# Weight splits of a float32 decoder trunk: low halves on GpSimd in four pieces, all high halves on ScalarE

## The chip, the cores and the metric

The kernel runs on one core of a Trainium2 chip. The metric is the device time of one execution in microseconds (us); the time given for a kernel is the median of its runs. Engines are named as in the profile: PE is TensorE's matmul and PEld its weight load, DVE is VectorE, ACT is ScalarE, POOL is GpSimd, SP is SyncE, which issues nearly all DMAs here.

## The reference

A decoder trunk of four layers on 256 tokens of width 1024, in float32. Each layer adds a token mixer and then a SwiGLU feed-forward network of inner width 2816 to the residual; a last RMS norm follows.

```
for i in range(4):
    h = rms_norm(x, norm_mix[i])
    x = x + (nsa, moba, short_conv)[i % 3](h)     # layers 0 and 3: nsa, 1: moba, 2: short_conv
    h = rms_norm(x, norm_ffn[i])
    x = x + (silu(h @ w_gate[i]) * (h @ w_up[i])) @ w_down[i]
return rms_norm(x, norm_final)
```

`nsa` is attention in three branches (compressed keys, selected blocks, sliding window) whose outputs are weighted by sigmoid gates; `moba` is causal block attention, which on 256 tokens is one block; `short_conv` is a gated convolution of width 3.

## The kernel before

**Numbers in two halves.** PE multiplies in float32r, a shorter form of float32. To keep float32's precision, a matrix X is held as a high half (X rounded to float32r) and a low half (X minus the high half), and a product is three matmuls: high by high, high by low, low by high. Activations are split by `split`, weights by `split_part`.

**The weight stream.** All weights lie in HBM in the order of their use, as about 400 parts of 128 x 1024 numbers (8 tiles of 128 x 128, 512 KB). SP loads a part into one of 4 buffers named `raw`. `split_part` (L94 to L114) makes the high half `whi` from `raw` by one copy (L112) and the low half `wlo` by one subtraction `raw - whi` (L113); there are 5 buffers of each. `take` (L116) hands out tiles and keeps the split of four further parts ahead of PE. A buffer of `raw` comes free for its next DMA when the low half is made, a buffer of `whi` or `wlo` when PE has read it. Parts of the step F, the compression weights of nsa, are loaded straight into a `whi` buffer (named `wf`) and not split.

**Who makes the halves.** Two tables, LO and HI, name the engine by the step that a part belongs to and its number modulo the length of the string: `a` is ACT, `v` is DVE, `p` is POOL. For steps that are in neither table (the feed-forward network, `conv`), the high half is made by ACT and the low half by DVE.

**Order of the work.** A scheduler orders the instructions of each engine when the program is built; each engine then runs its own list strictly in order and waits at the head of its list. In the mixers the list of steps (NSA_ORDER, MOBA_ORDER) mixes projections (`q`, `k`, `K`, `A`, `G`, `V`) with scores (`s`), transposes of probabilities (`T`) and the products with the values (`P`). Names that the rows show:

- L354 `row`: DVE scales a projection as it leaves PSUM. What comes next is a split into halves: ACT's cast, then DVE's subtraction (L182/L183 for moba's queries, L409/L410 for its keys, L558/L559 for nsa's queries, L530 to L533 for nsa's keys, where half of the subtractions are POOL's).
- L384, L387, L389, L391: the softmax: DVE's minimum, ACT's exponential, DVE's reciprocal, POOL's scaling `pr`. Then PE transposes `pr`, ACT and DVE split it (L182/L183 `pt`) and PE multiplies it with the values (L740 in nsa).
- L543: PE transposes the gates of nsa, which L354 has just written; L586 to L595: the gelu of nsa's compression; L606 `zk`: low half of the compressed keys, read by PE in L643; L663: a 128 x 16 product in the compressed softmax.
- L133 to L135, L343 to L345, L367 to L369, L153/L157: the matmuls with weights.
- L211: POOL sums squares for the RMS norm, a `tensor_tensor` of 128 x 256.

Of the kernel before, what the change touches and what calls it, by code (L numbers as in the profile page):

```python
# [9 lines left out]
F32 = mybir.dt.float32  # L10
F32R = mybir.dt.float32r
AF = mybir.ActivationFunctionType
OP = mybir.AluOpType
# [26 lines left out]
             "c1 s P T t1 s P T s P T P T P").split()  # L40
MOBA_ORDER = ("V0 k k V1 q q k k s s q q T s k q s P T k T P q s P T q q P T k s T k s P s P T T P P").split()
LO = {"V": "vp", "q": "vp", "nsa_out": "p", "moba_out": "vvvp", "G": "vvp", "K": "vp", "A": "vp", "moba_q": "p", "moba_V": "vp", "moba_k": "vvvp"}
HI = {"q": "aav", "A": "aav", "G": "aav", "K": "av", "nsa_out": "a", "moba_out": "v", "moba_k": "avv", "moba_V": "aav", "moba_q": "avv", "V": "a"}
OUT_BANKS = "AAAB"
CMP_BANK = "B"
GELU = "vector"
# [6 lines left out]
class Kernel:  # L53
# [40 lines left out]
    def split_part(self, q):  # L94
        nc = self.nc
        if self.names[q] == "F":
            t = self.operands.tile([P, PART * P], F32, tag="whi", name=f"wf{q}", bufs=W_BUFS)
            nc.sync.dma_start(t, self.ap["w"][q])
            self.parts[q] = (t, t)
            return  # L100
        if q not in self.raw:
            self.load_part(q)
        src = self.raw.pop(q)
        hi = self.operands.tile([P, PART * P], F32R, tag="whi", name=f"whi{q}", bufs=W_BUFS)
        lo = self.operands.tile([P, PART * P], F32R, tag="wlo", name=f"wlo{q}", bufs=W_BUFS)
        lo_eng, hi_eng = (e.get(self.names[q], d) for e, d in ((LO, "v"), (HI, "a")))
        eng = {"p": nc.gpsimd, "v": nc.vector}[lo_eng[q % len(lo_eng)] if q >= 4 else "v"]
        copy = {"a": nc.scalar.copy, "v": nc.vector.tensor_copy}[hi_eng[q % len(hi_eng)] if q >= 4 else "a"]
        n = PART * P // (2 if q < 4 else 1)
        for o in range(0, PART * P, n):  # L110
            c = slice(o, o + n)
            copy(hi[:, c], src[:, c])  # L112
            eng.tensor_tensor(out=lo[:, c], in0=src[:, c], in1=hi[:, c].bitcast(F32), op=OP.subtract)  # L113
        self.parts[q] = (hi, lo)  # L114

    def take(self, n=1):  # L116
# [860 lines left out]
```

## Time and profile before

| | us |
|---|---|
| median of 3 runs (lowest to highest) | 1284.33 (1282.88 to 1286.27) |
| profiled execution, its own time | 1285.58 |
| its span, first to last instruction | 1283.6 |

| engine | busy us in the span | share |
|---|---|---|
| PE matmul | 1242.1 | 97% |
| DVE | 900.2 | 70% |
| ACT | 652.7 | 51% |
| POOL | 306.8 | 24% |

The mean granted clock of PE is 0.991 of full speed. The span is the time from the first to the last instruction; the profiled execution's own time lies 1.98 us above it. Busy shares are means over stages: in the feed-forward networks PE has no gap at all, in the mixers it has some.

### The profile page before, as it was taken

The page shows a single profiled execution, that of the slowest core. Times are in us where ns is not written, and L with a number is a line of the kernel's source. Part 1 is how long each engine was busy: PE and PEld are TensorE (multiplying, and loading weights), DVE is VectorE, ACT ScalarE, POOL GpSimd, SP SyncE. Part 2 cuts the span into 40 slices and gives each one's busy share as a digit, 9 for nine tenths or more (in the row PEclk, how much of TensorE's full clock was granted, in tenths as well). Part 3 has the DMA queues.
Part 4 walks back from the last instruction along what each step waited for, and adds up shares of the span by engine and source line. Part 5 has one row for each costly group of instructions (what it writes and reads, how often), then busy time and mean ns, then how long its engine had stood idle before and what let it go on. Part 6 is the DMA issues. An engine that isn't in the chain of part 4 may idle for free.

```text
span 1283.6 us, 19976 instructions
## 1 busy us (share of the span) xinstructions
PE 1242.1 (97%) x7108; PEld 1086.2 (85%) x7108; DVE 900.2 (70%) x1655; ACT 652.7 (51%) x1197; POOL 306.8 (24%) x336
## 2 busy tenths in 40 slices
PE   8888999999999899999999999999998989999997
PEld 8877788888889888888899988888898878888886
DVE  7588886565768985656768786565867797756663
ACT  5368845454334644545434344454324797445542
POOL 2467620000356320000113110000334765000011
PEclk9999999999999999999999999999998999999999
DMA  8713066777664346766665656777665312677761
GB/s 274 242 59 115 16 207 189 218 219 219 192 181 144 102 126 194 237 201 213 217 184 176 197 183 198 212 221 224 188 183 192 100 50 60 210 207 225 221 214 55
DMA packets 91443, 226.72 MB, mean 177 GB/s; under 512 B 17488, under 2 KB 38352, under 8 KB 91344
## 3 DMA queue, kind: packets, MB, share of 16 engines
q1 hardware_dynamic: 91200, 225.41, 57.2%
q8 instruction: 56, 0.92, 0.3%
q14 instruction: 43, 0.35, 0.1%
q10 hardware_dynamic: 144, 0.04, 0.0%
HBM read 212.81 MB, written 1.05 MB: 167 GB/s over the span
## 4 chain that ended last, share of the span: by engine, by line
PE 85%; DVE 8%; ACT 3%; issue 2%; POOL 2%; DMA 1%; POOLq 0%; DVEq 0%; ACTq 0%
PE psA L153 14%; PE psA L157 7%; PE psB L343 6%; PE psB L345 6%; PE psB L344 6%; PE psA L344 5%; PE psA L343 5%; PE psA L345 5%; PE psA L133 4%; PE psA L134 4%; PE psA L135 4%; PE psB L153 2%; PE psB L579 2%; PE psC L345 2%; PE psC L343 2%
## 5 line engine op out<-in xcount | busy, mean ns | idle before, releaser
L112 ACT CAST whi<-raw 128x1024 fp32r<-128x1024 f32 (+1 forms) x356 | 369.5, 1039 | 425.4 <-PE psC L345 94.5
L113 DVE TENSOR_TENSOR wlo<-raw,whi 128x1024 fp32r<-128x1024 f32 (+1 forms) x338 | 412.4, 1226 | 238.8 <-ACT whi L112 224.4
L153 PE MATMUL psA<-ff,whi 128*128 128x512 f32 x840 | 229.2, 394 | 0.3 <-DVE ff L183 0.2
L211 POOL TENSOR_TENSOR ssq<-ssq,row 128x256 f32<-128x256 f32 x48 | 46.0, 958 | 547.9 <-issue 398.6
L153 PEld LDWEIGHTS psA<-ff,whi 128*128 128x128 f32 x840 | 149.4, 189 | 24.4 <-DVE ff L183 0.7
L133 PE MATMUL psA<-at,whi 128*128 128x256 f32 x536 | 154.9, 289 | 0.0
L135 PE MATMUL psA<-at,wlo 128*128 128x256 f32 x536 | 153.8, 287 | 0.0
L134 PE MATMUL psA<-at,whi 128*128 128x256 f32 x536 | 153.8, 287 | 0.0
L113 POOL TENSOR_TENSOR wlo<-raw,whi 128x1024 fp32r<-128x1024 f32 x52 | 127.3, 2453 | 82.8 <-ACT whi L112 52.2
L343 PE MATMUL psB<-whi,at 128*128 128x512 f32 x352 | 137.4, 390 | 0.0
L345 PE MATMUL psB<-whi,at 128*128 128x512 f32 x352 | 137.0, 389 | 0.0
L344 PE MATMUL psB<-wlo,at 128*128 128x512 f32 x352 | 136.9, 389 | 0.0
L157 PEld LDWEIGHTS psA<-ff,wlo 128*128 128x128 f32 x840 | 123.2, 190 | 11.1
L157 PE MATMUL psA<-ff,wlo 128*128 128x256 f32 x840 | 129.6, 282 | 0.0
L134 PEld LDWEIGHTS psA<-at,whi 128*128 128x128 f32 x536 | 104.7, 195 | 0.5
L133 PEld LDWEIGHTS psA<-at,whi 128*128 128x128 f32 x536 | 104.6, 195 | 0.5 <-DVE row L354 0.2
L135 PEld LDWEIGHTS psA<-at,wlo 128*128 128x128 f32 x536 | 104.5, 195 | 0.0
L343 PE MATMUL psA<-whi,at 128*128 128x512 f32 x256 | 99.6, 389 | 0.0
L344 PE MATMUL psA<-wlo,at 128*128 128x512 f32 x256 | 99.6, 389 | 0.0
L345 PE MATMUL psA<-whi,at 128*128 128x512 f32 x256 | 99.6, 389 | 0.0
L391 POOL TENSOR_SCALAR pr<-pr,rc,gates 128x256 f32<-128x256 f32 (+1 forms) x128 | 70.3, 563 | 40.2 <-DVE rc L389 34.1
L345 PEld LDWEIGHTS psB<-whi,at 128*128 128x128 f32 x352 | 66.1, 188 | 13.9
(215 smaller groups left out, 2084.6 us busy)
## 6 DMA issues: line engine op xcount, KB each, us to landing
raw<-in_w SPq DMA_DIRECT2D x384, 512.0 KB, 4.3
pt<-pt SPq DMA_DIRECT2D x320, 32.0 KB, 3.0
wf<-in_w SPq DMA_DIRECT2D x16, 512.0 KB, 4.4
h<-in_xt SPq DMA_DIRECT2D x4, 256.0 KB, 5.0
raw<-in_w SPq DMA_DIRECT2D x4, 256.0 KB, 5.1
pt<-pt SPq DMA_DIRECT2D x64, 16.0 KB, 3.1
out<-ff SPq DMA_DIRECT2D x4, 256.0 KB, 2.5
w<-in_w SPq DMA_DIRECT2D x2, 256.0 KB, 3.8
```

Of the source, the lines that this page charges most:

```text
L112: copy(hi[:, c], src[:, c])
L113: eng.tensor_tensor(out=lo[:, c], in0=src[:, c], in1=hi[:, c].bitcast(F32), op=OP.subtract)
L133: mm(out, wt[0], act[0], start=first, stop=False)
L134: mm(out, wt[0], act[1], start=False, stop=False)
L135: mm(out, wt[1], act[0], start=False, stop=last)
L153: mm(outs[o], w[0], acts[k].rearrange("p i s -> p (i s)"), start=(k == 0), stop=(k == n - 1))
L157: mm(outs[o][:, :S], w[1], acts[k][:, 0, :], start=False, stop=False)
L211: (nc.gpsimd if norm else nc.vector).tensor_tensor(out=self.ssq, in0=self.ssq, in1=sq, op=OP.add)
L343: mm(o, a[:, 0, s], hi, start=(k == 0), stop=False)
L344: mm(o, a[:, 0, s], lo, start=False, stop=False)
L345: mm(o, a[:, 1, s], hi, start=False, stop=(k == KT - 1))
L391: nc.gpsimd.tensor_scalar(pr[:, c], pr[:, c], rc[:, j:j + 1], gates[j], op0=OP.mult, op1=OP.mult)
```

## The change

The table HI goes, and every high half is made by ACT. A low half of POOL is made by four instructions of 256 columns in place of one of 1024; DVE's low halves stay whole. LO is unchanged, so which parts POOL makes is unchanged.

```diff
-HI = {"q": "aav", "A": "aav", "G": "aav", "K": "av", "nsa_out": "a", "moba_out": "v", "moba_k": "avv", "moba_V": "aav", "moba_q": "avv", "V": "a"}
+PIECES = 4
...
-        lo_eng, hi_eng = (e.get(self.names[q], d) for e, d in ((LO, "v"), (HI, "a")))
+        lo_eng = LO.get(self.names[q], "v")
         eng = {"p": nc.gpsimd, "v": nc.vector}[lo_eng[q % len(lo_eng)] if q >= 4 else "v"]
-        copy = {"a": nc.scalar.copy, "v": nc.vector.tensor_copy}[hi_eng[q % len(hi_eng)] if q >= 4 else "a"]
         n = PART * P // (2 if q < 4 else 1)
         for o in range(0, PART * P, n):
             c = slice(o, o + n)
-            copy(hi[:, c], src[:, c])
-            eng.tensor_tensor(out=lo[:, c], in0=src[:, c], in1=hi[:, c].bitcast(F32), op=OP.subtract)
+            nc.scalar.copy(hi[:, c], src[:, c])
+            m = n // (PIECES if eng is nc.gpsimd else 1)
+            for b in range(o, o + n, m):
+                d = slice(b, b + m)
+                eng.tensor_tensor(out=lo[:, d], in0=src[:, d], in1=hi[:, d].bitcast(F32), op=OP.subtract)
```

The lines below are moved by this: what is L113 before is L115 after, L354 is L356, and so on; the high half's copy is L112 before and L111 after. The scheduler also moves some rows against each other.

DVE in layer 3 (nsa), just ahead of the gates, first before, then after. The two casts are high halves; `wlo` is DVE's own low half.

```order
L112 CAST whi_9966<-raw_9964 128x1024
L533 TENSOR_TENSOR keys_109<-row_9944,keys_109 64x256
L113 TENSOR_TENSOR wlo_9983<-raw_9980,whi_9982 128x1024
L354 TENSOR_TENSOR row_10010<-psA_9979,rb_9723 128x256
L112 CAST whi_10032<-raw_10030 128x1024
L559 TENSOR_TENSOR ff_9978<-row_10010,ff_9978 64x256 x2
L113 TENSOR_TENSOR wlo_10033<-raw_10030,whi_10032 128x1024
L586 COPY pb_10044<-psB_9834 128x4
L589 TENSOR_TENSOR row_10046<-psB_9834,pb_10044 128x256
```
```order
L535 TENSOR_TENSOR keys_109<-row_10058,keys_109 64x256
L115 TENSOR_TENSOR wlo_10100<-raw_10097,whi_10099 128x1024
L356 TENSOR_TENSOR row_10127<-psA_10096,rb_9834 128x256
L561 TENSOR_TENSOR ff_10095<-row_10127,ff_10095 64x256 x2
L588 COPY pb_10164<-psB_9945 128x4
L115 TENSOR_TENSOR wlo_10153<-raw_10150,whi_10152 128x1024
L591 TENSOR_TENSOR row_10166<-psB_9945,pb_10164 128x256
```

Both casts are gone from DVE's list, and the copy `pb` now stands ahead of the low half instead of behind it.

DVE in layer 1 (moba), between two softmaxes, before and after: a reciprocal, two scaled projections and the low half of a key.

```order
L112 CAST whi_4380<-raw_4378 128x1024
L389 RECIPROCAL rc_4325<-den_4324 128x4
L354 TENSOR_TENSOR row_4370<-psA_4339,rb_3901 128x256
L410 TENSOR_TENSOR keys_106<-row_4370,keys_106 64x256 x2
L112 CAST whi_4466<-raw_4464 128x1024
L354 TENSOR_TENSOR row_4408<-psA_4377,rb_3901 128x256
```
```order
L391 RECIPROCAL rc_4412<-den_4411 128x4
L356 TENSOR_TENSOR row_4460<-psA_4426,rb_3964 128x256
L412 TENSOR_TENSOR keys_106<-row_4460,keys_106 64x256 x2
L356 TENSOR_TENSOR row_4501<-psA_4467,rb_3964 128x256
L386 ISA pr_4513,mn_4514<-psA_4505,mask 128x128
```

The two casts that stood ahead of the projections are gone.

POOL at about the same place in layer 1, before and after: the scaling of probabilities and POOL's low halves.

```order
L391 TENSOR_SCALAR pr_4186<-pr_4186,rc_4189 128x256 x2
L113 TENSOR_TENSOR wlo_4269<-raw_4266,whi_4268 128x1024
L391 TENSOR_SCALAR pr_4211<-pr_4211,rc_4214 128x128 x2
L391 TENSOR_SCALAR pr_4211<-pr_4211,rc_4214 128x256 x2
L113 TENSOR_TENSOR wlo_4343<-raw_4340,whi_4342 128x1024
L113 TENSOR_TENSOR wlo_4381<-raw_4378,whi_4380 128x1024
```
```order
L393 TENSOR_SCALAR pr_4270<-pr_4270,rc_4273 128x256 x2
L393 TENSOR_SCALAR pr_4295<-pr_4295,rc_4298 128x128 x2
L393 TENSOR_SCALAR pr_4295<-pr_4295,rc_4298 128x256 x2
L115 TENSOR_TENSOR wlo_4353<-raw_4350,whi_4352 128x256 x4
L115 TENSOR_TENSOR wlo_4430<-raw_4427,whi_4429 128x256 x4
```

Each low half is a row of four, and the second set of probabilities has moved ahead of a low half that it stood behind.

## Rows read from the trace of the kernel before

**Rows 1.** Busy time of the engines in chosen stretches. Columns: from:to, length, then PE, PEld, DVE, ACT and POOL busy us with the number of instructions, granted clock as a share of 2.4 GHz, share of the DMA engines, GB/s. The first is the feed-forward network of layer 0, the second the moba mixer with its keys, queries and softmaxes, the last four are all the stretches between the start and the tail of the program in which the granted clock is 0.50.
```profile
165.00:320.00 155.00, 155.00 (x737) 130.30 (x736) 100.68 (x126) 76.25 (x96) 4.29 (x6) 1.00 0.69 210
380.00:475.00 95.00, 89.33 (x620) 81.56 (x618) 84.15 (x193) 48.47 (x135) 40.61 (x47) 1.00 0.42 123
60.10:63.50 3.40, 3.13 (x15) 3.13 (x16) 1.72 (x5) 0.58 (x2) 0.00 (x0) 0.50 0.77 276
73.70:77.10 3.40, 3.40 (x20) 3.40 (x18) 0.61 (x5) 2.20 (x10) 1.95 (x4) 0.50 0.35 135
981.70:988.50 6.80, 5.54 (x26) 5.54 (x27) 4.13 (x9) 4.01 (x7) 0.02 (x1) 0.50 0.71 231
1009.00:1012.40 3.40, 3.40 (x12) 2.69 (x10) 2.79 (x10) 2.26 (x10) 2.44 (x6) 0.50 0.00 0
```

**Rows 2.** Waits of PE, longest in total first: engine and line waited for, us in total, times, longest us.
```profile
PE psB L543 <- DVE row L354: 6.7, 2, 3.4
PE psA L367 <- DVE mn L384: 3.3, 2, 2.4
PE psC L740 <- ACT pr L387: 3.0, 2, 1.6
PE psB L464 <- DVE pt L183: 2.7, 1, 2.7
PE psB L643 <- DVE zk L606: 1.9, 1, 1.9
PE psA L705 <- DVE row L354: 1.6, 1, 1.6
PE psA L449 <- DVE row L354: 1.6, 1, 1.6
PE psB L722 <- POOL pr L391: 0.9, 4, 0.3
```

**Rows 3.** Groups of instructions by line, and for three of them the duration in ns as minimum/median/maximum.
```profile
L112 ACT CAST whi<-raw 128x1024 fp32r<-128x1024 f32 x348 | 364.7, 1048 | 424.5 <-PE psC L345 94.5 <-DMA raw<-in_w 75.0 <-PE psA L345 66.0
L112 DVE CAST whi<-raw 128x1024 fp32r<-128x1024 f32 x34 | 33.7, 992 | 19.3 <-issue 4.9 <-PE psA L153 4.3 <-PE psA L134 4.2
L112 DVE CAST whi<-raw x34: 675/694/2612, 19.3 to 1011.4; 128x1024 fp32r<-128x1024 f32 x34
L113 POOL TENSOR_TENSOR wlo<-raw,whi x52: 2351/2404/3397, 20.1 to 1080.1; 128x1024 fp32r<-128x1024 f32 x52
L211 POOL TENSOR_TENSOR ssq<-ssq,row x48: 731/742/2603, 163.4 to 1268.1; 128x256 f32<-128x256 f32 x48
```

**Rows 4.** Timeline of layer 3 ahead of the gates (DVE, POOL, PE): start, us, engine, line, operation, in brackets the idle time before it and what ended it.
```profile
974.29 2.21 DVE L112 CAST whi<-raw 128x1024 fp32r<-128x1024 f32 x1 [1.19 <-PE psB L579]
977.43 3.32 DVE L113 TENSOR_TENSOR wlo<-raw,whi 128x1024 fp32r<-128x1024 f32 x1
977.24 2.42 POOL L113 TENSOR_TENSOR wlo<-raw,whi 128x1024 fp32r<-128x1024 f32 x1 [1.30 <-ACT whi L112]
982.96 0.69 PE L543 MATMUL psB<-ident,row 128*128 128x128 f32 x2 [3.30 <-DVE row L354]
```

**Rows 5.** Timeline of layer 0 ahead of the compressed scores (DVE, POOL, PE); L559 stands for two instructions.
```profile
69.50 3.04 DVE L559 TENSOR_TENSOR ff<-row,ff 64x256 fp32r<-64x256 f32 x2
69.89 2.36 POOL L113 TENSOR_TENSOR wlo<-raw,whi 128x1024 fp32r<-128x1024 f32 x1
72.85 0.86 PE L643 MATMUL psB<-ff,zk 128*128 128x256 f32 x5 [1.90 <-DVE zk L606]
```

**Rows 6.** Timeline of moba (DVE, POOL, PE); L410 stands for two instructions.
```profile
408.25 2.61 DVE L112 CAST whi<-raw 128x1024 fp32r<-128x1024 f32 x1
411.79 2.41 DVE L410 TENSOR_TENSOR keys<-row,keys 64x256 fp32r<-64x256 f32 x2 [0.53 <-ACT keys L409]
407.92 2.40 POOL L113 TENSOR_TENSOR wlo<-raw,whi 128x1024 fp32r<-128x1024 f32 x1
419.69 0.33 PE L464 MATMUL psB<-ident,pr 128*128 128x128 f32 x1 [2.67 <-DVE pt L183]
```

**Rows 7.** Timeline of layer 3's compressed softmax (DVE, POOL, PE).
```profile
1001.71 2.14 DVE L663 TENSOR_TENSOR cmx<-cmx,gates 128x16 f32<-128x16 f32 x1
1001.43 2.38 POOL L113 TENSOR_TENSOR wlo<-raw,whi 128x1024 fp32r<-128x1024 f32 x1
1007.78 0.47 PE L367 MATMUL psA<-whi,at 128*128 128x512 f32 x1 [2.43 <-DVE mn L384]
```

**Rows 8.** Timeline of layer 0 at the values (DVE, POOL).
```profile
93.37 3.08 DVE L113 TENSOR_TENSOR wlo<-raw,whi 128x1024 fp32r<-128x1024 f32 x1
92.95 2.42 POOL L113 TENSOR_TENSOR wlo<-raw,whi 128x1024 fp32r<-128x1024 f32 x1
95.31 3.40 POOL L113 TENSOR_TENSOR wlo<-raw,whi 128x1024 fp32r<-128x1024 f32 x1
```

**Rows 9.** Timeline of layer 0 ahead of the gates (DVE, POOL).
```profile
57.54 2.44 DVE L592 TENSOR_TENSOR row<-row,row 128x256 f32<-128x256 f32 x1
57.21 2.49 POOL L113 TENSOR_TENSOR wlo<-raw,whi 128x1024 fp32r<-128x1024 f32 x1 [0.99 <-ACT whi L112]
```

**Rows 10.** Timeline of layer 0's first low half of POOL, and PE's first matmul that reads it.
```profile
20.08 2.41 POOL L113 TENSOR_TENSOR wlo<-raw,whi 128x1024 fp32r<-128x1024 f32 x1 [2.20 <-DVE whi L112]
24.64 0.28 PE L135 MATMUL psA<-at,wlo 128*128 128x256 f32 x1
```

## The prediction

> **What bounds the kernel now.** I read the stretches first. In the feed-forward networks PE is busy without a gap, 155.00 of 155.00 us [rows 1]: a change to the splits gains nothing there as long as the halves stay ahead. So only PE's waits count, and the list of waits is the second view. No row of it names L113, and L112 is named only at the very start of the program: PE never waits for a weight half in the mixers. It waits for small DVE instructions of the mixers: the gates' projection (6.7 us in two waits), the softmax minimum (3.3), a transposed probability (2.7), the compressed keys (1.9) and two projections (1.6 each) [rows 2]. The third view is the granted clock: four stretches of 3.40, 3.40, 6.80 and 3.40 us stand at 0.50, that is 1.2 instead of 2.4 GHz, and in each PE had just waited 1.9 us or longer. PE was busy 3.13, 3.40, 5.54 and 3.40 us there, which at the full clock would have been half: 1.6, 1.7, 2.8 and 1.7 us lost, 7.8 in all [rows 1].
>
> The timelines then show why those small instructions were late. In each place DVE stood still until a low half of POOL had ended:
> - Layer 3, gates: DVE's own low half starts at 977.43, POOL's ends at 977.24 + 2.42 = 979.66, DVE's at 980.75. It waited 2.23 us and worked 1.09. PE's transpose of the gates came 3.30 us late [rows 4].
> - Layer 0, compressed keys: the pair L559 ends at 72.54, 0.29 us behind POOL's end at 72.25; PE waited 1.90 [rows 5].
> - moba: a DVE cast takes 2.61 us from 408.25 while POOL works until 410.32; the pair L410 behind it takes 2.41; PE waited 2.67 at 419.69 [rows 6].
> - Layer 3, compressed softmax: a product of 16 columns takes 2.14 us, ending 0.04 us behind POOL; PE waited 2.43 [rows 7].
> - Layer 0, gates: L592 takes 2.44 us and ends 0.28 us behind POOL's end at 59.70 [rows 9].
>
> So a DVE instruction that reads two operands from SBUF, or a DVE cast, does not run beside a low half of POOL; it waits up to a whole one, 2.40 us at the median. The Trainium skill says the same ("SBUF — State Buffer", section "Who interferes with whom"): the pair of ports that the two share is held for the whole instruction. By that rule a wait shrinks to one piece when the instruction is cut; the trace agrees for uncut ones, and no run here shows cut ones.
>
> **What the change costs and gives, on the profiled execution's own 1285.58 us.**
>
> *The pieces.* The trace has no 256-column low half; nearest is POOL's sum of squares on 128 x 256, 742 ns at the median [rows 3]. Bounds: a quarter of 2404 ns, 601 ns, if nothing is fixed per instruction; 742 ns if the fixed part is that of L211. I take 742, the same kind of operation on the same size: four make 2.97 us, and some 0.1 to 0.2 us between them makes 3.1. A low half of POOL takes 0.7 us longer (0 to 0.8), 52 times. As PE waits for none of them, that reaches the end only through what stands behind on POOL, the scaling `pr`: 0.9 us in four waits now [rows 2]. I charge 2 us, three waits longer by 0.7.
>
> *DVE's wait.* Between two low halves of POOL that stand back to back, DVE does get in: its low half of 93.37 waits for POOL's first one (end 95.37), ends at 96.45, and POOL's second one, started at 95.31, takes 3.40 instead of 2.40 [rows 8]. So DVE waits at most for the rest of one piece, 0.74 us, half of that on average, instead of up to 2.4. A run of several such DVE instructions pays this each time while the four pieces last, so single stragglers gain most.
>
> *The casts.* 34 casts leave DVE, 694 ns each at the median and 992 in the mean with the waits, 33.7 us in all [rows 3]; moba, where DVE is busy 84.15 of 95.00 us, loses the most of them [rows 1]. They go to ACT at 1048 ns, 35.6 us. In that stretch ACT is busy 48.47 of 95.00, and its casts start when PE frees the buffer, as DVE's did. Bounds: nothing, if ACT's idle time covers all; half of a cast, 0.5 us, for each of some 15 casts in the softmax stretches, 8 us, if every one stands ahead of a waited-for exponential. I take 2 us: ACT is now waited for in 3.0 us at L740 [rows 2], and few of the casts stand there.
>
> *Place by place*, with what is late next:
> - Layer 3, gates: the 2.21 us cast is gone, and the wait of 2.23 becomes at most 0.74. Then POOL's next low half meets the gelu once or twice. PE's 3.30 becomes about 0.7: -2.6. The clock's 6.80 us stretch begins inside that wait; without it -2.8.
> - Layer 0, keys: 1.90 becomes 0.4, -1.5; the clock stretch behind it, -1.7.
> - moba: waits of 1.6 and 2.67 become 0.3 and 0.7, -3.3: three casts and three waits for POOL lie in the chain ahead of them, and next come the exponentials.
> - Layer 3, compressed softmax: 2.43 becomes 1.3, as the four DVE instructions behind the 16 columns now meet pieces: -1.1, and half of the clock's 1.7, -0.8, as the rest of the wait may still drop it.
> - Layer 0, L705: DVE's low half of 93.37 ends about 1.3 us sooner; 1.6 becomes 0.5, -1.1.
> - Layer 0, gates: DVE's low half, L591 and L592 alternate with eight pieces of two low halves; 3.4 becomes 2.6, -0.8, and the clock falls as before.
> - The other wait for L384, 0.9 us: a cast of DVE stood in its chain; -0.7.
>
> Sum: 11.1 us of waits and 5.3 us of clock, -16.4. Against it +2 for `pr`, +2 for ACT, and +2 for the rows of PE, DVE and ACT that the scheduler moved at the end of moba and in nsa, which I can't price from rows: +6. Net -10.4: 1275.2 for an execution like the profiled one. That one lies 1.25 above the median of the runs, so I say 1274.
>
> **The rivals.**
> *POOL leaves no room between pieces of one low half.* The two low halves of rows 8 are different parts, each with waits of its own; four pieces of one part have nothing to wait for. If POOL keeps the ports through all four, DVE waits for 3.1 us instead of 2.4, the five places that hang on a single wait lose 0.7 each with no clock gained, +3.5, and only the casts are saved, about -5 in moba and at layer 3's gates: 1284.3 - 1.5, 1283. Against it, the rows: POOL's second instruction was already started at 95.31 and still let DVE through. The Trainium skill ("GPSIMD Engine Reference", section "Instruction dispatch") says that each of GpSimd's cores goes on to the next instruction as soon as its own share is done, which is the way this rival would come about; no run here shows it for pieces.
>
> *ACT becomes what is late.* At the upper bound of 8 us for the casts, with 6 us of it above what I charged, the gain is 4 us: 1280 to 1281.
>
> *Slower: POOL gets behind with its low halves.* If DVE takes the ports at each of the three seams of a part with a low half of its own (1.09 us), a part takes 3.1 + 3.3 = 6.4 us, 4.0 more than now. The tightest place is the first: POOL ends at 22.49, PE reads at 24.64, 2.15 us later [rows 10]. So PE would wait up to 1.9 us, and the buffer `raw` would come back as late. It decides where DVE has a low half ready at every seam and PE takes parts fast, in the projections of both nsa layers: about six parts of POOL there, +11, against -3 that remain in moba: 1292. Against it: PE reads a part tile by tile and needs the last piece latest, and DVE's list there mixes low halves with operands from PSUM.
>
> **How the numbers follow.** A measurement of this kernel tells a change from none at about 0.3%, 3.9 us. Chances: the forecast 0.72, its own range 1266 to 1280; no room between the pieces 0.10; ACT late 0.09; POOL behind 0.09. The range that holds 8 of 10 runs from 1264 (all the named waits and all of the clock gone, nothing charged: 11.1 and more from waits, 7.8 from the clock, -20) to 1284, which takes in the two middle rivals and leaves POOL behind out. Faster by over 0.3%: the forecast and a part of ACT late, 0.75; within 0.3%: 0.16; slower 0.09.
>
> **What the changed kernel's profile would show.** 208 low halves of POOL near 742 ns, none of DVE's low halves above about 2.0 us (3.3 before), no DVE cast at L111; L663, L592 and the pair L559 each under 1.2 us; PE's wait for the gates in layer 3 under 1 us; two stretches or fewer at 0.50 between start and tail. I am wrong if DVE's single instructions still last 2 us or more (no room), if ACT leads the list of PE's waits, or if PE waits for L115.

## The result, and the profile after

The changed kernel takes 1274.23 us at the median (1273.67 to 1274.99, four runs) against 1285.01 before (1282.88 to 1286.27, four runs, the three given ahead among them): 0.9924 of it, with a 95% interval of 0.9908 to 0.9939. Forecast were 1274 us. The profiled execution took 1274.58 us with a span of 1272.8, before 1285.58 and 1283.6.

The stretches first, in the columns of [rows 1]: the feed-forward network of layer 0, moba, and all the stretches between start and tail in which the granted clock is one half.

```profile
165.00:320.00 155.00, 155.00 (x733) 130.18 (x732) 100.47 (x128) 77.39 (x99) 4.20 (x6) 1.00 0.70 216
380.00:475.00 95.00, 90.77 (x595) 81.19 (x594) 75.14 (x182) 60.88 (x147) 42.99 (x69) 0.98 0.40 121
109.40:112.80 3.40, 3.40 (x13) 3.21 (x14) 3.40 (x15) 3.25 (x9) 2.90 (x6) 0.51 0.03 5
413.20:416.60 3.40, 3.40 (x18) 3.40 (x18) 3.28 (x6) 1.73 (x6) 0.11 (x1) 0.50 0.73 251
996.90:1000.30 3.40, 3.40 (x9) 2.62 (x9) 2.69 (x13) 3.25 (x14) 1.95 (x4) 0.50 0.04 17
```

PE is still busy without a gap in the feed-forward network. The second stretch can't be set beside that of [rows 1] as it stands: moba begins 7.4 us sooner now, so the same times of the span hold other work. The whole mixer, from moba's first matmul to the first of the feed-forward network behind it (764 matmuls in both), before and after:

```profile
353.58:475.00 121.42, 115.75 (x764) 104.58 (x762) 102.25 (x216) 57.21 (x149) 54.70 (x53) 1.00 0.45 133
346.19:468.86 122.67, 118.44 (x764) 106.12 (x763) 84.53 (x197) 75.63 (x168) 62.41 (x98) 0.99 0.44 134
```

DVE has lost 17.7 us with its 19 casts of moba, and ACT has gained 18.4; yet the mixer takes 1.3 us longer. Three stretches are left at 1.2 GHz, 10.2 us in all instead of 17.0, and two of them, at 109.4 and 413.2, stand where there was none before.

PE's waits, as in [rows 2] (the wait for the first weights at the start left out):

```profile
PE psC L742 <- ACT pr L389: 3.4, 2, 2.1
PE psA L369 <- DVE mn L386: 2.5, 2, 1.8
PE psB L466 <- DVE pt L185: 2.2, 1, 2.2
PE psB L545 <- DVE row L356: 1.6, 2, 0.8
PE psA L707 <- DVE row L356: 1.2, 2, 0.9
PE psA L451 <- DVE mn L386: 1.0, 1, 1.0
PE psA L704 <- POOL keys L535: 1.0, 1, 1.0
```

The gates' projection (L545) went from 6.7 us to 1.6 and is no longer first; the compressed keys' wait for DVE (L606 before) has left it. The transposed probability in moba (L466) has hardly moved, and the wait for ACT's exponentials is now the longest.

The splits themselves, two groups with their durations as minimum/median/maximum and one with busy time and mean:

```profile
L115 DVE TENSOR_TENSOR wlo<-raw,whi x338: 674/1225/1831, 12.0 to 1250.1; 128x1024 fp32r<-128x1024 f32 x165, 128x512 fp32r<-128x512 f32 x4
L115 POOL TENSOR_TENSOR wlo<-raw,whi x208: 723/739/1729, 20.6 to 1072.7; 128x256 fp32r<-128x256 f32 x104
L115 POOL TENSOR_TENSOR wlo<-raw,whi 128x256 fp32r<-128x256 f32 x208 | 157.8, 792 | 61.8 <-ACT whi L111 52.0 <-issue 7.1 <-DVE row L591 1.5
```

A piece takes 739 ns at the median, as taken from the sum of squares [rows 3], and 792 in the mean, as some pieces wait for DVE in their turn. No low half of DVE lasts above 1.83 us (3.32 before).

Two places in the timeline (start, duration, engine, line, operation; in brackets the idle time before it). Layer 3 at the gates, to set beside [rows 4]:

```profile
972.06 2.34 POOL L115 TENSOR_TENSOR wlo<-raw,whi 128x256 fp32r<-128x256 f32 x3 [1.45 <-DVE row L591]
972.98 0.83 DVE L594 TENSOR_TENSOR row<-row,row 128x256 f32<-128x256 f32 x1
973.74 0.41 DVE L356 TENSOR_TENSOR row<-psA,rb 128x256 f32<-128x256 f32 x1
974.21 0.33 PE L545 MATMUL psB<-ident,row 128*128 128x128 f32 x1 [0.81 <-DVE row L356]
```

This went as forecast: the gelu's product starts beside a piece and waits for that piece alone (0.83 us with its own work), and PE waits 0.81 instead of 3.30. moba did not:

```profile
395.72 5.61 POOL L115 TENSOR_TENSOR wlo<-raw,whi 128x256 fp32r<-128x256 f32 x8
396.03 5.57 DVE L185 TENSOR_TENSOR ff<-row,ff 128x256 fp32r<-128x256 f32 x1 [0.23 <-ACT ff L184]
411.51 0.33 PE L466 MATMUL psB<-ident,pr 128*128 128x128 f32 x1 [2.19 <-DVE pt L185]
```

One DVE instruction of 0.42 us of work stands for 5.57 us until eight pieces, two whole parts, are through. There were seven ends of a piece at which it could have gone ahead. PE's two waits of moba, 1.03 and 2.19 us, and the clock's stretch at 413.2 come behind it. It is the longest of its kind, and rare: 48 `tensor_tensor` instructions of DVE with both inputs in SBUF start while a piece runs. 44 of them get in at the first end of a piece, two at the second (they had started 0.01 and 0.05 us before the first), one at the third, and this one at the eighth.

### The profile page after: what moved, and what is told of

It reads as the page before. It is cut to its first block, busy times and chain, and to the rows that moved or that the text cites. A ratio compares the mean times of both kernels' runs of the same rounds, so it can differ in the third digit from the quotient of the medians.

```text
span 1272.8 us, 20178 instructions
## 1 busy us (share of the span) xinstructions
PE 1239.8 (97%) x7108; PEld 1082.7 (85%) x7108; DVE 861.0 (68%) x1621; ACT 686.5 (54%) x1231; POOL 334.0 (26%) x492
## 4 chain that ended last, share of the span: by engine, by line
PE 85%; DVE 6%; ACT 4%; issue 3%; POOL 1%; DMA 0%; POOLq 0%; SPq 0%; DVEq 0%; ACTq 0%
PE psA L155 15%; PE psA L159 8%; PE psB L345 6%; PE psB L347 6%; PE psB L346 6%; PE psA L346 5%; PE psA L345 5%; PE psA L347 5%; PE psA L135 4%; PE psA L136 4%; PE psA L137 4%; PE psB L581 2%; PE psB L155 2%; PE psC L347 2%; PE psC L345 2%
## 5 line engine op out<-in xcount | busy, mean ns | idle before, releaser
L111 ACT CAST whi<-raw 128x1024 fp32r<-128x1024 f32 (+1 forms) x390 | 405.2, 1040 | 451.4 <-PE psC L347 97.4
L115 DVE TENSOR_TENSOR wlo<-raw,whi 128x1024 fp32r<-128x1024 f32 (+1 forms) x338 | 410.9, 1221 | 265.2 <-ACT whi L111 246.2
L115 POOL TENSOR_TENSOR wlo<-raw,whi 128x256 fp32r<-128x256 f32 x208 | 157.8, 792 | 61.8 <-ACT whi L111 52.0
L389 ACT ACTIVATE pr<-pr,mn 128x128 f32<-128x128 f32 (+1 forms) x160 | 71.4, 450 | 13.7 <-DVE mn L386 12.8
```

Of the source, the lines that this page charges most:

```text
L111: nc.scalar.copy(hi[:, c], src[:, c])
L115: eng.tensor_tensor(out=lo[:, d], in0=src[:, d], in1=hi[:, d].bitcast(F32), op=OP.subtract)
L389: nc.scalar.activation(pr[:, c], pr[:, c], AF.Exp, bias=mn[:, j:j + 1], scale=-1.0, accum_out=den[:, j:j + 1])
```

## The experiments

PE's longest idle times at eight places, from each kernel's timeline in us; a dash is under 0.15. The last rows are the sum of all of PE's idle times above 0.15 us without the start, the length of moba's mixer from its first matmul to the first behind it, and the number of stretches at 1.2 GHz between start and tail.

| place (line of the changed kernel) | before | changed | pieces alone | casts alone | two pieces | eight pieces |
|---|---|---|---|---|---|---|
| layer 0, gates (L545) | 3.42 | 0.81 | 3.24 | 0.40 | 0.64 | 0.50 |
| layer 0, compressed keys (L645 for DVE) | 1.90 | 0.28 | 0.29 | 1.90 | 0.83 | - |
| layer 0, scores (L707) | 1.60 | 0.86 | - | 2.48 | 1.39 | 0.57 |
| layer 0, weighing (L742 for ACT's pr) | 1.64 | 2.06 | 2.07 | 1.63 | 1.78 | 0.82 |
| moba, scores (L451) | 1.58 | 1.03 | - | 0.43 | 0.40 | 1.40 + 1.03 |
| moba, turning (L466) | 2.67 | 2.19 | 0.27 | 0.88 | 0.49 | 1.79 |
| layer 3, gates (L545) | 3.30 | 0.81 | 1.59 | 1.70 | 1.44 | 0.65 |
| layer 3, compressed softmax (L369) | 2.43 | 1.81 | 1.81 | 2.44 | 2.28 | 1.26 |
| all | 28.0 | 19.0 | 19.8 | 20.4 | 19.4 | 19.5 |
| moba's mixer, its length | 121.4 | 122.7 | 118.2 | 119.1 | 118.7 | 123.6 |
| stretches at 1.2 GHz | 4 | 3 | 2 | 2 | 1 | 1 |

**Pieces alone.** The kernel before with

```diff
-            eng.tensor_tensor(out=lo[:, c], in0=src[:, c], in1=hi[:, c].bitcast(F32), op=OP.subtract)
+            m = n // (PIECES if eng is nc.gpsimd else 1)
+            for b in range(o, o + n, m):
+                d = slice(b, b + m)
+                eng.tensor_tensor(out=lo[:, d], in0=src[:, d], in1=hi[:, d].bitcast(F32), op=OP.subtract)
```

> The kernel before with POOL's low halves in four pieces, the high halves' table as it was (34 casts stay on DVE). Theory (DVE gets in between pieces): the waits on a single DVE instruction shrink from up to 2.4 us to at most 0.74, so the gates of layer 3, the compressed keys of layer 0 and the compressed softmax of layer 3 give most of what they gave in the changed kernel; moba keeps the part that hangs on DVE's casts. 1276 to 1279 us, 0.993 to 0.996 of before. Rival (no room between the pieces): a low half holds DVE for 3.1 us instead of 2.4, so 1285 to 1289 us, and the whole gain of the changed kernel is the casts'.

Measured: 1272.93 us, 0.9919 of before (0.9901 to 0.9937). The pieces alone bring the whole gain, more than the theory said, and the rival is out as the general case. moba has no wait above 0.5 us: the gain that was to come from the casts came from the pieces. Layer 0's gates keep their wait, though, for they hang on a load as well as on POOL. Before (POOL, SyncE's issue of the load, ACT, DVE, PE):

```profile
47.68 3.23 POOL L113 TENSOR_TENSOR wlo<-raw,whi 128x1024 fp32r<-128x1024 f32 x1 [1.65 <-issue]
50.94 0.33 SPq L91 DMA_DIRECT2D raw<-in_w  x1
54.67 1.05 ACT L112 CAST whi<-raw 128x1024 fp32r<-128x1024 f32 x1 [0.93 <-DMA raw<-in_w]
55.75 1.55 DVE L113 TENSOR_TENSOR wlo<-raw,whi 128x1024 fp32r<-128x1024 f32 x1 [1.39 <-ACT whi L112]
60.37 0.48 PE L543 MATMUL psB<-ident,row 128*128 128x128 f32 x1 [3.42 <-DVE row L354]
```

and with pieces alone (lines one to four higher):

```profile
46.59 5.09 POOL L117 TENSOR_TENSOR wlo<-raw,whi 128x256 fp32r<-128x256 f32 x4 [1.65 <-issue]
55.32 1.05 ACT L113 CAST whi<-raw 128x1024 fp32r<-128x1024 f32 x1 [3.63 <-DMA raw<-in_w]
56.40 1.23 DVE L117 TENSOR_TENSOR wlo<-raw,whi 128x1024 fp32r<-128x1024 f32 x1 [3.03 <-ACT whi L113]
57.86 0.85 DVE L596 TENSOR_TENSOR row<-row,row 128x256 f32<-128x256 f32 x1
59.10 0.33 PE L547 MATMUL psB<-ident,row 128*128 128x128 f32 x1 [3.24 <-DVE row L358]
```

In both DVE stands with nothing to do but a low half whose cast waits for the load, and the gelu's instructions are queued behind it. Before, that is 1.39 us, and another 2.0 are L592 standing still beside POOL (2.44 us [rows 9] for 0.43 of work). With pieces alone the second part shrinks to 0.4 us (0.85), but the first grows to 3.03: DVE now gets in between the four pieces, so that they take 5.09 us, and the load waits for the last of them.

**Casts alone.** The changed kernel with `PIECES = 1`.

> The changed kernel with POOL's low halves in one piece again: all casts on ACT. Theory: moba and the gates of layer 3 gain (3 to 5 us with their share of the clock), the compressed keys of layer 0 and the compressed softmax of layer 3 keep their waits of about 2 us and their clock stretches: 1279 to 1282 us, 0.995 to 0.998. Rival (no room between the pieces): the casts are the whole gain, 1273 to 1276 us, 0.991 to 0.993.

Measured: 1275.55 us, 0.9938 (0.9918 to 0.9957), a gain of 8.2 us where the theory expected 2 to 5. By its number this is the rival's, but the kernel beside it, with pieces alone, excludes the rival; it is the theory's sizes that fall. The compressed keys and the compressed softmax keep their waits, as it said, but layer 0's gates lose theirs:

```profile
45.91 1.22 DVE L115 TENSOR_TENSOR wlo<-raw,whi 128x1024 fp32r<-128x1024 f32 x1 [1.11 <-ACT whi L111]
47.16 0.33 SPq L91 DMA_DIRECT2D raw<-in_w  x1
53.74 1.80 DVE L115 TENSOR_TENSOR wlo<-raw,whi 128x1024 fp32r<-128x1024 f32 x1 [0.52 <-ACT whi L111]
56.59 0.33 PE L545 MATMUL psB<-ident,row 128*128 128x128 f32 x1 [0.40 <-DVE row L356]
```

The seventeenth load of raw weights in order of time, which went out at 50.94 before, when a low half of POOL had ended, goes out at 47.16, when one of DVE has ended, 1.6 us sooner than before. Why another low half releases it, the rows don't show. L594, the L592 of before, then takes 0.43 us, as no low half of POOL runs beside it. So 8.2 and 10.8 us are not two parts of one sum; casts and pieces remove largely the same waits, and both together give 10.8.

**Two pieces.** `PIECES = 2`.

> The changed kernel with POOL's low halves in two pieces of 512 columns. From 742 ns at 256 columns and 2404 at 1024 a piece takes about 1.3 us. Theory: DVE waits for at most 1.3 us instead of 0.74, PE's waits lie between those of one piece and of four: 1275 to 1279 us. Rival (DVE is kept out by a second piece that is queued already): like one piece, and the time is that of the casts alone.

Measured: 1271.78 us, 0.9910 (0.9892 to 0.9929), better than the theory's range. The single waits do lie between those of one piece and of four (keys 0.83, softmax 2.28), but moba loses its waits, since the instruction that starved gets in after one piece (four of them, two parts):

```profile
395.18 5.24 POOL L115 TENSOR_TENSOR wlo<-raw,whi 128x512 fp32r<-128x512 f32 x4
395.57 1.18 DVE L185 TENSOR_TENSOR ff<-row,ff 128x256 fp32r<-128x256 f32 x1 [0.22 <-ACT ff L184]
```

**Eight pieces.** `PIECES = 8`.

> The changed kernel with eight pieces of 128 columns. By the same two durations a piece takes about 0.46 us and a low half 3.7 us. Theory: DVE waits at most 0.46 us, POOL's scaling of the probabilities comes later by another 0.7 us in two or three waits: 1271 to 1276 us, within 0.3% of the changed kernel. Rival (DVE is kept out as long as pieces stand queued): waits of 4 to 7 us in moba, 1278 us or more.

Measured: 1272.76 us, 0.9910 (0.9889 to 0.9932). The time is the theory's (one of the six runs took 1267.62 us, the others 1271.78 to 1274.30; why is not known). In the traces both are borne out, in different places: the keys' wait is gone, layer 0's weighing waits 0.82 instead of 2.06, and in moba the same instruction waits for all sixteen pieces:

```profile
393.48 6.73 POOL L115 TENSOR_TENSOR wlo<-raw,whi 128x128 fp32r<-128x128 f32 x16
393.79 6.70 DVE L185 TENSOR_TENSOR ff<-row,ff 128x256 fp32r<-128x256 f32 x1 [0.47 <-ACT ff L184]
```

**Moba's query weights in two pieces**, the others in four.

```diff
-PIECES = 4
+PIECES = {"moba_q": 2}
...
-            m = n // (PIECES if eng is nc.gpsimd else 1)
+            m = n // (PIECES.get(self.names[q], 4) if eng is nc.gpsimd else 1)
```

> The changed kernel, but the parts of moba's query weights (all of their low halves are POOL's) in two pieces of 512 columns, every other low half of POOL in four. Theory (in the changed kernel two of these parts stood back to back as eight pieces of 256 and kept one DVE instruction of moba out for 5.57 us; two pieces of 512 let it in at the first seam, as in the kernel with two pieces): that instruction takes 1.3 us or less, the waits of PE at 403.58 (1.03 us) and 411.51 (2.19 us) shrink to 0.4 and 0.5, and the clock's stretch at 413.2 is gone (1.7): 4 us less than the changed kernel, 1270 us. Rival (the long instruction is not what costs moba its gain, but the casts that now stand on ACT ahead of the exponentials): the waits stay, 1273 to 1275 us.

Measured: 1270.50 us, 0.9898 (0.9884 to 0.9911). The theory holds:

```profile
395.92 5.25 POOL L115 TENSOR_TENSOR wlo<-raw,whi 128x512 fp32r<-128x512 f32 x4
396.31 1.19 DVE L185 TENSOR_TENSOR ff<-row,ff 128x256 fp32r<-128x256 f32 x1 [0.21 <-ACT ff L184]
```

Its waits in moba are 0.50 and 0.52 us and the stretch at 413 is gone, with every cast still on ACT. So the starved instruction, not the casts on ACT, had cost moba its gain: 2.6 to 3.7 us, by the two medians of the changed kernel (1273.1 in the last run below). Its mixer takes 118.8 us, after 122.7 and 121.2 in the two profiles of the changed kernel.

**Moba's casts shared out as before**, four pieces everywhere.

```diff
+HI = {"moba_out": "v", "moba_k": "avv", "moba_V": "aav", "moba_q": "avv"}
...
-            nc.scalar.copy(hi[:, c], src[:, c])
+            copy(hi[:, c], src[:, c])
```

where `copy` is DVE's for "v" and ACT's for "a" and for all other weights.

> The changed kernel with four pieces everywhere, and the high halves of moba's weights shared out between ACT and DVE as in the kernel before; nsa's stay on ACT. Theory of the starved instruction: with some casts on DVE POOL no longer gets two whole parts of moba at once, as in the kernel with pieces alone, whose moba had no wait of PE above 0.5 us: 1269 to 1271 us. Rival of the casts on ACT: the same time, but here with the casts gone from ACT's list as the cause; it is told from the theory by the kernel beside it that keeps the casts on ACT and has moba's query weights in two pieces. If neither holds, moba gains nothing: 1273 to 1276 us.

Measured: 1270.81 us, 0.9898 (0.9881 to 0.9914), with no wait above 0.5 us in moba. With DVE making some casts in its own order, POOL is no longer handed two whole parts at that place: two pieces stand between two sets of probabilities, and the instruction takes 0.57 us.

**Moba's casts shared out as before, with eight pieces in nsa.**

> As the kernel beside it (moba's casts shared out as before, moba in four pieces), with eight pieces of 128 columns for POOL's low halves in nsa. From the traces of the kernel with eight pieces (layer 0's mixer 9.5 us shorter than before, against 7.1 with four) and of the one with pieces alone (moba 3.6 us shorter): if stages add up, 1267 to 1269 us. Rival (what one stage gains shifts the next): 1270 to 1273 us.

Measured: 1269.11 us, 0.9886 (0.9871 to 0.9902): at the upper end of what the sum of the stages gives, 1.7 us below the kernel beside it, with ranges that just overlap.

**All low halves on DVE.** `LO = {}`: POOL makes none, and all casts stay on ACT.

> No low half on POOL: all 52 of them go to DVE, all casts stay on ACT. It shows what the standing still costs against the work itself. Theory: no DVE instruction of the mixers lasts longer than its own work any more (48 us of such time in the changed kernel, 68 before), but DVE takes on 52 x 1.18 = 61 us of low halves, and moba, where it was busy 84 of 95 us before, is bound by DVE: 1280 to 1295 us. Rival (standing still was as costly as the work): 1270 to 1276 us, and POOL's help is worth nothing.

Measured: 1267.98 us, 0.9879 (0.9864 to 0.9894), the fastest kernel of the study; both expectations were too slow. moba's whole mixer and DVE's low halves:

```profile
345.73:462.96 117.23, 115.91 (x764) 104.39 (x762) 91.47 (x212) 74.61 (x168) 19.66 (x38) 1.00 0.46 137
L115 DVE TENSOR_TENSOR wlo<-raw,whi x390: 690/1225/1753, 11.5 to 1243.3; 128x1024 fp32r<-128x1024 f32 x191, 128x512 fp32r<-128x512 f32 x4
```

In moba DVE makes 31 low halves, after 16 in the changed kernel; they keep it busy 36.8 us instead of 19.7, 17.1 more, but in all it is busy only 6.9 us more, 91.47 instead of 84.53. Over the span it is 896.8 us instead of 861.0: 52 low halves of 1.2 us are 62 us, and some 26 of them come back as time in which DVE no longer stands still. What I had not seen is that such time was part of the busy 84.15 us of [rows 1], which I had read as work. The Trainium skill ("Perfetto Trace Analysis", section "Optimizing Scalar/DVE Operations") warns that moving operations between these two engines might not help, as they share a port; this run agrees, with 1268.0 us for no low half on POOL against 1274.2 for 52.

**All low halves on DVE, the casts shared out as before.** `LO = {}` in the kernel before.

> All low halves on DVE, none on POOL, and the high halves shared out between ACT and DVE as in the kernel before: set beside the kernel with all low halves on DVE and all casts on ACT (1268.0 us) it prices the casts alone, with nothing of POOL's low halves in DVE's way. Theory (away from POOL a cast costs DVE its own 0.7 us, and DVE has room for that outside moba): 34 x 0.7 = 24 us more on DVE, of which at most a few reach PE: 1267 to 1272 us. Rival (the casts on DVE were a cost of their own, as the prediction charged them): 1274 us or more. Third case (the casts on ACT are what is late now): 1266 us or less.

Measured: 1268.65 us, 0.9883 (0.9868 to 0.9898). As the theory said: away from POOL's low halves the place of the casts makes 0.7 us, no difference that can be told. The cast itself takes the same 694 ns at the median as in [rows 3], but its longest is 1.17 us instead of 2.61:

```profile
L112 DVE CAST whi<-raw x34: 673/694/1174, 19.1 to 995.1; 128x1024 fp32r<-128x1024 f32 x34
346.83:464.14 117.31, 115.71 (x763) 104.49 (x762) 102.78 (x231) 57.14 (x149) 22.15 (x38) 1.00 0.44 136
```

This kernel differs from the kernel before in LO alone, so the two price POOL's help by itself: it costs 14.5 us (1283.14 to 1268.65). The last line is moba's mixer: DVE makes 15 low halves more in it and is busy as long as before, 102.78 after 102.25 us. Over the span it takes on 62 us of work and is busy 16.4 us more (916.6 after 900.2). How much of the 14.5 us comes from DVE no longer standing still, and how much from buffers of `raw` that come free sooner (1.2 us a low half instead of 2.4), no run separates.

**The changed kernel again.**

> The changed kernel once more, unaltered. If the long DVE instruction of moba (5.57 us beside eight pieces) comes from the order of the program, it is there again, within 0.3 us of the same length, with PE's waits of 1.0 and 2.2 us behind it; if it is chance, DVE gets in after one or two pieces in this execution, and moba is some 4 us shorter in it. The median should be 1274 us either way within 1 us if it is the program's order; if it is chance, single executions should spread over 4 us.

Measured: 1273.12 us, 0.9922 (0.9908 to 0.9935). The long instruction is there to the hundredth, and PE's wait behind it; the clock is not:

```profile
396.37 5.58 DVE L185 TENSOR_TENSOR ff<-row,ff 128x256 fp32r<-128x256 f32 x1 [0.21 <-ACT ff L184]
411.85 0.33 PE L466 MATMUL psB<-ident,pr 128*128 128x128 f32 x1 [2.19 <-DVE pt L185]
413.20:416.60 3.40, 3.40 (x30) 3.35 (x29) 3.21 (x7) 2.05 (x6) 0.46 (x2) 1.00 0.71 257
```

Starving is set by the program, then. The five runs lie between 1272.41 and 1275.23 us. The granted clock behind the same wait was 0.50 in one execution and 1.00 in the other, and so it was behind the softmax's wait of 1.8 us in layer 3. This execution has one stretch at 1.2 GHz, at 110.7, where the first had three, and its span is 1.9 us shorter.

## Why the prediction came out, point by point

The mechanism is shown: DVE instructions with two operands in SBUF, and DVE's casts, stood still beside POOL's low halves. Cutting these, taking the casts away, or having no low half on POOL each gains, and the first two gain mostly the same time. At layer 0's gates a late load had a share that the prediction left out. The net sum was right, 11.0 us between the profiled executions for 10.4 forecast; several of its terms were not.

- **The pieces' duration**: 742 ns taken, 739 measured. But I added 0.1 to 0.2 us between them, and there is nothing between: eight take 5.61 us, 0.70 each, as each starts some 0.04 us before the one ahead of it ends. A part of four pieces takes 2.8 us where DVE leaves it alone, 0.4 longer than a whole one. With the turns that DVE now takes in between it is 3.08 in the mean after 2.45, so the 0.7 charged came out near (0.63), for another reason.
- **Layer 3's gates** (-2.6 and -2.8 of clock): -2.5, and the 6.80 us stretch is gone. Right.
- **Layer 0's keys** (-1.5 and -1.7): -1.6, and the stretch is gone. Right; the pieces alone do it.
- **Layer 0's gates** (-0.8, clock as before): -2.6, and the stretch behind is gone too. The step that failed is its cause. I read the 2.44 us of L592 [rows 9] as the wait; standing still there was some 2.0 us of it, and 1.4 were DVE's wait for a load that went out late, which I had not traced. The casts' move took both away, the pieces alone only the first: 0.40 us with casts alone, 3.24 with pieces alone.
- **moba** (-3.3): 4.25 us of waits became 3.22, -1.0, and a stretch of the clock that cost 1.7 was added (in the first execution, not in the second). The step that failed is "DVE waits at most for the rest of one piece". The rival of no room between pieces is real at this one place, and I had priced it as a rule for all of them. In the kernels of the table in which this instruction got in, moba's two waits are 0.3 to 1.3 us together.
- **Layer 3's softmax** (-1.1 and half a stretch): -0.6. The 16 columns take 0.49 instead of 2.14 us [rows 7], but the minima behind them still come late. **L707** (-1.1): -0.7. **The other wait for the minimum** (-0.7): -0.2.
- **The +6 charged**: PE's waits for POOL's probabilities in nsa are 1.0 us after 0.9 [rows 2], so +2 there was too much. The wait for ACT's exponentials grew from 3.0 to 3.4 us, but with the casts still on DVE it grows as much (2.07 at the weighing with pieces alone, 1.63 with casts alone): it is the pieces' cost, a DVE instruction that took 2.00 us at 104.46 across two ends, not ACT's. New is 0.6 us more for POOL's keys (L704).

PE's waits fell by 9.0 us, and the clock's loss from the 7.8 of [rows 1] to 5.1, half of the 10.2 us in which PE was busy throughout: 11.7 together. The span fell by 10.8, so that all the rest, the moved rows among it, cost 0.9. That the forecast met the median within 0.3 us is partly luck: layer 0's gates gave 3.4 us more than said, clock included, and moba 4 less.

Of the promised signs, the 208 pieces, DVE's longest low half, the absence of casts and the gates of layer 3 are there. Three failed: single instructions of 2.00 and 5.57 us, three stretches at 1.2 GHz in the first execution (one in the second), and the pair L561 at 1.42 us for a promised 1.2. Two of the three signs of being wrong came: DVE's single instructions of 2 us and more, and ACT at the head of PE's waits (3.4 us at L742). The first is the rival of no room between pieces, at two places. The second is not the rival of ACT being late: the wait of 2.07 us at the weighing is there with pieces alone, the casts on DVE. The rival of POOL getting behind is no general case, as no kernel's list of waits names a low half of POOL; at one place it is real, at layer 0's gates with pieces alone, where four pieces took 5.09 us and the load behind them came late.

## What to carry to other kernels

A busy DVE beside a busy GpSimd is not the sum of its work: before moving elementwise work to GpSimd to relieve DVE, look for DVE instructions that last far above their own median (a cast of 0.69 us that took 2.61), for such time counts as busy, and then run the kernel with the work back on DVE. Here that cost DVE 16.4 us of busy time for 62 us of work, none of it in moba, and the kernel was 14.5 us faster. If GpSimd must do it, cut its instructions to what the waiting engine can afford, and look in the trace for single instructions that still wait through a whole row of them. Two edits aimed at the same waits don't add up, so price them one at a time, and trace a late engine back through its casts and loads before calling it locked out.

## What the runs showed of the hardware that was not expected

- DVE mostly gets in at the end of the GpSimd instruction that it meets (44 of 48 in the changed kernel), but not always. The Trainium skill ("SBUF — State Buffer", section "Who interferes with whom") has the port pair held for the whole instruction; the 44 agree with it. But one DVE instruction waited for eight of them in a row (5.57 us) and, with smaller ones, for sixteen (6.70). At the same place four instructions of 512 columns let it in after the first. What decides it is open: satisfied waits, as between the two parts, did not open a gap, and scaled probabilities of POOL stood ahead of the pieces in both cases.
- GpSimd's instructions of 128, 256, 512 and 1024 columns took 461, 739, 1292 and 2404 ns at the median: some 185 ns and 2.17 ns a column, with rows of them 0.04 us shorter for each seam.
- The granted clock can fall behind a given wait in one execution of a kernel and stay up in the next (2.19 us of idle PE, clock 0.50 and 1.00), so a single profile prices a stretch, not the place. Whether the two ran on the same chip is not known here; within the four runs of the result the mean granted clock varies too, from 0.995 to 0.997.
